# Merge turned round: the ungated sums of the two-input branch first, with Strassen pairs, the gated branch last; HGRN gates at the head of the late stage

## The chip, the cores and the metric

The kernel runs on one core of a Trainium2 chip. TensorE (PE) multiplies matrices; VectorE (DVE), ScalarE (ACT) and GpSimd (POOL) work on tiles in the on-chip memory; SyncE (SP) and POOL issue most of the DMA transfers. Time is device time of one launch, in microseconds (us). The kernel before took 2472.12 us, the median of three runs (2466.22, 2472.12 and 2474.85).

## The reference

One layer of a hybrid decoder step is computed, for 1024 prompt positions and 8 samples. From a normalised input h come the columns of an HGRN2 branch, of a Mamba-2 branch (SSD), and two planes of merge gates. What matters here is the end of the two branches and their merge (cut from the reference):

```python
o_hg = _rmsnorm(o_hg, p['hg_norm']) * jax.nn.silu(og)
...
y = y.reshape(Bsz, T, SSM_INNER) * jax.nn.silu(z)
y = _rmsnorm(y.reshape(Bsz, T, SSM_GROUPS, SSM_INNER // SSM_GROUPS), p['ssm_norm'])
...
u = (jax.nn.sigmoid(ga + bma) * (o_hg @ p['w_br_a'])
     + jax.nn.sigmoid(gb + bmb) * (y @ p['w_br_b']))
x = x + g1 * (u @ p['w_out'])
...
x = x + g2 * (jnp.square(jax.nn.relu(h2 @ p['w_up'])) @ p['w_down'])
```

D_MODEL is 1024, SSM_INNER is 2048: o_hg has 1024 features, y has 2048, and so `w_br_b` has twice the inputs of `w_br_a`.

## The kernel before

**Planes.** Activations lie transposed: a plane is 128 features on the partitions by NT = 1032 positions (1024 and 8). A matrix of 1024 features is KD = 8 planes, y is 16. Each operand is split into a high and a low part (`hi`, `lo`; `wh`, `wl` for weights), and a product is three matmuls: high by low, low by high, high by high. The split costs an ACT copy and a DVE subtraction for each plane and each weight block.

**Two ways to multiply.** `dense` makes one output plane from 8 input planes: 3 column parts of 344, times 8 planes, times 3 matmuls, 72 in all (line 90). `strassen_pair` makes two output planes from 8 input planes in 7 products of half size instead of 8: 7 products, 2 column quarters of 258, 4 planes, 3 matmuls, 168 in all (line 1314). It needs sums of quarters of the input (`T`, made once for several pairs by `differences` and a split) and sums of quarters of the weights (`strassen_weights`, line 1259, for each pair), and its evacuations add a kept product to another on DVE. `DenseK` makes one or two planes with the input planes in the outer loop, so that it can start before all of them are there.

**Late stage.** `phase_late` makes, from h, the HGRN output gates `og` (8 planes) and the SSD gates `z` (16 planes) in twelve Strassen pairs, in the order og, z, z, four times over; then one pair and one block of merge gates. Beside each pair, the pair before it is finished: `og_post` multiplies o by a row scale (`ybc`, broadcast from DRAM, line 1165) and by silu(og) (line 1166), and stores o to `od` (line 1167). `z_post` multiplies y by silu(z) (line 1176), makes a row scale, and one pair later applies it and stores y to `yd` (line 1190). The loads of o, ybc and y, and the stores of od, are issued by POOL (lines 1200, 1201, 1208). They use the six buffers of pool E, of which the `T` planes hold two; og, z and the merge gates use the four of pool D.

**Merge.** `phase_merge` starts with the gated branch `w_br_a`: 8 planes, each multiplied into a sigmoid gate `u` (line 962), the first two by one `DenseK` that takes planes of o as they come. Then come the 8 planes of the first half of `w_br_b` and the 8 of the second half (lines 990 and 991: gate times sum, added to `u`), the first two of the second half again by a `DenseK`. 24 output planes, all dense; every `w_br_b` sum is multiplied by its gate when it leaves PSUM, in both halves. `phase_out` multiplies by `w_out`.

**Feed-forward.** `phase_ffn` has a down projection of four chunks of 8 input planes. Chunks 0 to 2 are 3 dense planes, two Strassen pairs and 1 dense plane each; meanwhile the operand sums are made from planes loaded a second time (`operands`), and the planes of the next chunk are loaded and split (`load_split_in`, lines 925 to 927) ahead of the last dense plane.

**What sets the order.** The program is written in one thread; a scheduler keeps each engine's order by priorities (`high_priority(AHEAD)` moves weight loads, weight splits and evacuations ahead). An engine works through its queue in that order and waits at an instruction whose input is not there, with all behind it. Buffers come from pools with a fixed number of tiles for each tag (`LATE` maps tags to pools); a load waits until the former user of its buffer is done.

Of the kernel before, what the change touches and what calls it, by code (L numbers as in the profile page):

```python
# [7 lines left out]
F32 = mybir.dt.float32  # L8
# [9 lines left out]
P = 128  # L18
T = 1024
# [899 lines left out]
def load_split_in(k, src, tag):  # L919
# [5 lines left out]
    nc.sync.dma_start(raw, src)  # L925
    nc.scalar.activation(hi, raw, AF.Copy)
    nc.vector.tensor_tensor(lo, raw, hi.bitcast(F32), op=ALU.subtract)
    return hi, lo
# [26 lines left out]

def phase_merge(k):

    nc = k.nc
    u, y1, y2, gb = [], [], [], []

    def mul(m):
        return lambda s, ps: nc.vector.tensor_tensor(u[m][:, cs(s)], u[m][:, cs(s)], ps, op=ALU.mult)
    raw = [k.pp.tile([P, NT], F32, tag="L", name="or") for _ in range(4)]
    with k.tc.high_priority(AHEAD):
        for i in range(4):
            nc.sync.dma_start(raw[i], k.od[i])
    d = DenseK(k, (k.i["w_br_a"][0], k.i["w_br_a"][1]), (mul(0), mul(1)))
    oX = []
    for i in range(KD):
        with k.tc.high_priority(AHEAD):  # L970
            oX.append(split_plane(k, raw[i], "A") if i < 4 else load_split(k, k.od[i], "A"))
            if i == 7:
                k.kept = k.hi
                k.late()
            if i == 3:
                u += [load_gate(k, m, "Q1", k.hi) for m in range(2)]
        d.step(*oX[i])
    for m in range(2, KD):
        u.append(load_gate(k, m, "Q1", k.hi if m < 4 else None))
        dense(k, k.i["w_br_a"][m], oX, mul(m))  # L980
        y1.append(load_split(k, k.yd[m - 2], "Q3" if m < 6 else "Q2"))
    y1 += [load_split(k, k.yd[m], "Q2") for m in range(6, KD)]
    for m in range(KD):
        gb.append(load_gate(k, KD + m, "A"))
    order(k, nc.scalar.preload_act_table_set("natural_log_exp_and_others"), k.sigmoid)

    def evac1(m):
        def f(s, ps):
            t = k.sp2.tile([P, SW], F32, tag="mt", name="mt", bufs=2)
            nc.vector.tensor_tensor(t, gb[m][:, cs(s)], ps, op=ALU.mult)  # L990
            nc.vector.tensor_tensor(u[m][:, cs(s)], u[m][:, cs(s)], t, op=ALU.add)
        return f
    for m in range(KD):
        dense(k, k.i["w_br_b"][m], y1, evac1(m))
        if m < 4:
            y2.append(load_split(k, k.yd[KD + m], "A"))
    uX = []
    for m in range(KD):
        tag = "Q3" if m < 4 else "A"
        hi = k.pp.tile([P, NT], F32R, tag=tag, name="uh")  # L1000
        lo = k.pp.tile([P, NT], F32R, tag=tag, name="ul")
        uX.append((hi, lo))

    def evac2(m):
        add = evac1(m)
        hi, lo = uX[m]

        def f(s, ps):
            add(s, ps)
            uu = u[m][:, cs(s)]  # L1010
            nc.scalar.activation(hi[:, cs(s)], uu, AF.Copy)
            nc.vector.tensor_tensor(lo[:, cs(s)], uu, hi[:, cs(s)].bitcast(F32), op=ALU.subtract)
        return f
# [43 lines left out]
def phase_out(k, uX):  # L1057
# [3 lines left out]
    for m in range(KD):  # L1061
        x1.append(k.pp.tile([P, NT], F32, tag="Q1", name="x1"))
        nc.sync.dma_start(x1[m], k.i["xT"][m])
    h2 = []
    for m in range(KD):
        tag = "A" if m < 4 else "Q2"
        h2.append((k.pp.tile([P, NT], F32R, tag=tag, name="h2h"),
                   k.pp.tile([P, NT], F32R, tag=tag, name="h2l")))
# [31 lines left out]
def late_planes(k, T, i):  # L1100

    nc = k.nc
    a, b = [k.pp.tile([P, NT], F32, tag="D", name=n) for n in ("ta", "tb")]
    for x, (xh, xl) in ((a, k.hX[i]), (b, k.hX[i + 4])):
        nc.vector.tensor_tensor(x, xh.bitcast(F32), xl.bitcast(F32), op=ALU.add)
    differences(k, a, b)
    for x, ts in ((a, (1, 3)), (b, (4, 2))):
        p = split_plane(k, x, "T", "th", "tl")
        for n, t in enumerate(ts):
            T[t].append(tuple(y[:, n * HN:(n + 1) * HN] for y in p))  # L1110
# [9 lines left out]
def phase_late(k, gates):  # L1120
# [74 lines left out]
    for n in range(12):  # L1195
        if n % 3 == 0:
            j = n // 3
            og, o, ybc = planes("D", "og"), planes("E", "o"), planes("E", "ybc")
            for a in range(2):
                nc.gpsimd.dma_start(o[a], k.od[2 * j + a])  # L1200
                nc.gpsimd.dma_start(ybc[a], k.rh[2 * j + a].broadcast_to([P, NT]))
            strassen_pair(k, [k.i["w_hg"][(2 * j + a) * 4 + 1] for a in range(2)], X, pair(og))
            beside(k, og_post(og, j, o, ybc))
        else:
            g = n // 3 * 2 + n % 3 - 1
            z, y = planes("D", "z"), planes("E", "y")
            for a in range(2):
                nc.gpsimd.dma_start(y[a], k.yd[2 * g + a])
            strassen_pair(k, [k.i["w_ssm"][g * 6 + 4 + a] for a in range(2)], X, pair(z))
            beside(k, z_post(z, g, y))  # L1210
# [5 lines left out]
    finish(k)  # L1216
    gate_block(k, next(gates), "D", True)
# [3 lines left out]
def strassen_planes(k, h2, T, i):  # L1221

    nc = k.nc
    a, b = stage(k), stage(k)
    for x, (xh, xl) in ((a, h2[i]), (b, h2[i + 4])):
        nc.vector.tensor_tensor(x, xh.bitcast(F32), xl.bitcast(F32), op=ALU.add)  # L1230
    differences(k, a, b)
    for x, tag, ts in ((a, "A", (1, 3)), (b, "Q3", (4, 2))):
# [97 lines left out]
def phase_ffn(k, x1, h2):  # L1330
# [55 lines left out]
    spare = []  # L1386

    def shape(c):
        return 3, 2 if c < 3 else 0

    def operands(c, T, i):
        tags = "A%d" % (c % 2), "Q3" if c % 2 else "Q2"
        if i == 0:
            spare[:] = [[k.pp.tile([P, NT], F32, tag=t, name="ar") for t in tags] for _ in range(2)]
        ps = [[k.pp.tile([P, NT], F32R, tag=t, name=n) for n in ("th", "tl")] for t in tags]
        raw = spare[i % 2] if i < 3 else [stage(k) for _ in ps]
        for n, r in enumerate(raw):
            nc.sync.dma_start(r, ad[c * KD + i + 4 * n])
        differences(k, *raw)
        for (hi, lo), r, ts in zip(ps, raw, ((1, 3), (4, 2))):  # L1400
            nc.scalar.activation(hi, r, AF.Copy)
            nc.vector.tensor_tensor(lo, r, hi.bitcast(F32), op=ALU.subtract)
            for n, t in enumerate(ts):
                T[t].append(tuple(y[:, n * HN:(n + 1) * HN] for y in (hi, lo)))

# [12 lines left out]
    for c in range(4):  # L1418
        T = {n: [] for n in (1, 2, 3, 4)}
        ahead, pairs = shape(c)  # L1420
        for m in range(ahead):
            for i in ((0, 1), (2,), (3,))[m] if pairs else ():
                operands(c, T, i)
            dense(k, down[c * KD + m], aX, add(m))
        X = strassen_operands(aX, T) if pairs else None
        for n in range(pairs):
            m = ahead + 2 * n
            strassen_pair(k, [down[c * KD + m + a] for a in range(2)], X, add_pair(m))
        if c == 3:
            break  # L1430
        nX = [act(c + 1, i) for i in range(KD)]
        for m in range(ahead + 2 * pairs, KD):
            dense(k, down[c * KD + m], aX, add(m), 2)
        aX = nX
    M0 = 3
    free = [k.pp.tile([P, NT], F32R, tag=t, name="free") for t in ("A1", "Q3") for _ in range(8)]
# [20 lines left out]
LATE = {"A": ("A0",) * 8 + ("A1",) * 8, "T": ("L",) * 14 + ("E",) * 2, "Q1": ("L",) * 8, "Q2": ("D",) * 4 + ("E",) * 4, "Q3": ("E",) * 2 + ("L",) * 6}  # L1457
# [22 lines left out]
def body(ctx, tc, ins, outs):  # L1480
# [30 lines left out]
    with tc.tile_pool(name="pl", bufs=1) as pl, tc.tile_pool(name="sp2", bufs=1) as k.sp2:  # L1511
        k.pp.add(pl, L=14)
# [122 lines left out]
```

## Time and profile before

| What | Value |
|---|---|
| runs (median) | 2466.22, 2472.12, 2474.85 (2472.12) us |
| the profiled execution: time | 2468.79 us |
| its span | 2466.9 us |
| granted TensorE clock, mean | 0.997 |
| late stage's thirteen pairs | from 1106.7 to 1386.2 us |
| merge's planes of `w_br_a` after its first two, and of the first half of `w_br_b` | from about 1423.5 us on |
| feed-forward's chunk passage, used as a pattern | 2171 to 2192 us |

The time of the profiled execution is the one that sums from the trace stand against; it lies 3.3 us below the median. A busy share is the engine's busy time over the span. In rows of a timeline stand the start, the duration, engine, line, operation, output and inputs, and in brackets how long the engine was idle before and what released it; "L90" is line 90 of the kernel before.

### The profile page before, as it was taken

What the parts mean: (1) busy time and instruction counts of PE and PEld (TensorE: products, weight loads), DVE (VectorE), ACT (ScalarE), POOL (GpSimd) and SP (SyncE); (2) the same over time, 40 slices, a digit from 0 to 9 for tenths busy, and PEclk for the clock granted to TensorE, in tenths of its full rate; (3) what the DMA queues carried; (4) which work ended last, traced back from release to release, by engine and by line L of the source; (5) the groups of instructions that cost most, each with busy time, mean ns of one, the idle gap of its engine ahead of it and who ended that gap; (6) DMA issues with size and microseconds to landing.
All of it is one profiled execution on the core that took longest, in us unless ns stands there. A gap on an engine that the chain in (4) does not pass through costs nothing.

```text
span 2466.9 us, 51549 instructions
## 1 busy us (share of the span) xinstructions
PE 2429.1 (98%) x21918; PEld 2365.5 (96%) x21918; DVE 1685.2 (68%) x2953; ACT 1118.9 (45%) x1789; POOL 112.7 (5%) x218
## 2 busy tenths in 40 slices
PE   8999999999999999999999999999999999999998
PEld 7999999999999999999999999999999999999997
DVE  7656666459888788886777644356976666786755
ACT  4444454466665556535556523123533334343331
POOL 0000000000000000000111000000012222000000
PEclk9999999999999999999999999999999999999999
DMA  6333333334545454533555744223333335354231
GB/s 262 122 114 122 107 117 112 123 93 148 174 131 172 142 166 130 186 127 112 181 189 181 249 138 154 69 103 130 99 106 104 106 107 181 124 189 152 81 129 70
DMA packets 111591, 339.39 MB, mean 138 GB/s; under 512 B 20128, under 2 KB 26128, under 8 KB 111344
## 3 DMA queue, kind: packets, MB, share of 16 engines
q1 hardware_dynamic: 94656, 283.23, 34.3%
q0 software_dynamic: 16272, 52.52, 6.1%
q8 instruction: 172, 2.82, 0.5%
q14 instruction: 59, 0.48, 0.1%
q10 hardware_dynamic: 432, 0.35, 0.0%
HBM read 266.45 MB, written 69.85 MB: 136 GB/s over the span
## 4 chain that ended last, share of the span: by engine, by line
PE 84%; DVE 5%; DMA 4%; ACT 3%; issue 3%; POOL 0%; DVEq 0%; ACTq 0%; POOLq 0%
PE acc L90 55%; PE b L1314 17%; PE lv_ps L587 2%; PE y_ps L882 1%; PE kvx_ps L849 1%; PE o_ps L551 1%; PE yi_ps L890 1%; PE acc L141 1%; DMA y<-yd 1%; DMA wr<-od 1%; DVE wl L58 1%; PE ada_ps L205 1%; PE kv_ps L534 1%; DVE wl L1259 1%; PE cb_ps L812 1%
## 5 line engine op out<-in xcount | busy, mean ns | idle before, releaser
L90 PE MATMUL acc<-hl,wh 128*128 128x344 f32 x1608 | 527.6, 328 | 0.1
L90 PE MATMUL acc<-hh,wl 128*128 128x344 f32 x1608 | 516.5, 321 | 0.0
L90 PE MATMUL acc<-hh,wh 128*128 128x344 f32 x1608 | 515.6, 321 | 0.0
L90 PEld LDWEIGHTS acc<-hl,wh 128*128 128x128 f32 x1608 | 302.3, 188 | 5.2 <-issue 2.8
L90 PEld LDWEIGHTS acc<-hh,wh 128*128 128x128 f32 x1608 | 302.5, 188 | 3.9 <-issue 3.9
L90 PEld LDWEIGHTS acc<-hh,wl 128*128 128x128 f32 x1608 | 302.6, 188 | 0.0
L90 PE MATMUL acc<-hi,wl 128*128 128x344 f32 (+3 forms) x888 | 285.2, 321 | 1.9 <-DVE wl L58 1.8
L1314 PE MATMUL b<-th,wl 128*128 128x258 f32 x992 | 281.4, 284 | 5.6 <-DVE wl L1259 5.4
L90 PE MATMUL acc<-lo,wh 128*128 128x344 f32 (+3 forms) x888 | 283.8, 321 | 1.4 <-ACT wh L57 1.4
L90 PE MATMUL acc<-hi,wh 128*128 128x344 f32 (+3 forms) x888 | 284.2, 320 | 0.0
L1314 PE MATMUL b<-tl,wh 128*128 128x258 f32 x992 | 280.4, 283 | 0.0
L1314 PE MATMUL b<-th,wh 128*128 128x258 f32 x992 | 280.2, 283 | 0.0
L57 ACT ACTIVATE wh<-wr 128x1024 fp32r<-128x1024 f32 (+1 forms) x146 | 151.0, 1037 | 218.9 <-PE acc L90 148.3
L58 DVE TENSOR_TENSOR wl<-wr,wh 128x1024 fp32r<-128x1024 f32 (+1 forms) x146 | 175.2, 1201 | 69.2 <-ACT wh L57 68.2
L1314 PEld LDWEIGHTS b<-th,wl 128*128 128x128 f32 x992 | 187.6, 189 | 7.9 <-DVE wl L1259 7.4
L1259 DVE TENSOR_TENSOR wl<-wr,wh 128x512 fp32r<-128x512 f32 (+1 forms) x155 | 139.8, 902 | 77.8 <-ACT wh L1277 45.0
L1314 PEld LDWEIGHTS b<-tl,wh 128*128 128x128 f32 x992 | 187.4, 189 | 4.5 <-issue 4.5
L1314 PEld LDWEIGHTS b<-th,wh 128*128 128x128 f32 x992 | 187.4, 189 | 0.0
L90 PEld LDWEIGHTS acc<-hi,wl 128*128 128x128 f32 x888 | 167.3, 188 | 4.3 <-DVE wl L58 3.3
L90 PEld LDWEIGHTS acc<-lo,wh 128*128 128x128 f32 x888 | 167.0, 189 | 3.4 <-ACT wh L57 2.0
L90 PEld LDWEIGHTS acc<-hi,wh 128*128 128x128 f32 x888 | 167.5, 189 | 0.7
L756 DVE SCALAR_TENSOR_TENSOR cv<-raw,cst,cv 128x1024 f32<-128x1024 f32 x96 | 122.5, 1276 | 0.5
(346 smaller groups left out, 5129.6 us busy)
## 6 DMA issues: line engine op xcount, KB each, us to landing
wr<-w_ssm SPq DMA_DIRECT2D x48, 512.0 KB
wr<-w_ada SPq DMA_DIRECT2D x36, 512.0 KB
lo<-ad SPq DMA_DIRECT2D x32, 516.0 KB
wr<-w_hg SPq DMA_DIRECT2D x32, 512.0 KB
w<-cumd SPq DMA_DIRECT2D x32, 512.0 KB
wr<-w_up SPq DMA_DIRECT2D x32, 512.0 KB
wr<-w_down SPq DMA_DIRECT2D x32, 512.0 KB
ad<-r POOLq DMA_DIRECT2D x96, 129.0 KB, 2.2
```

Of the source, the lines that this page charges most:

```text
L57: nc.scalar.activation(wh[:, c], wr[:, c], AF.Copy)
L58: nc.vector.tensor_tensor(wl[:, c], wr[:, c], wh[:, c].bitcast(F32), op=ALU.subtract)
L90: last = nc.tensor.matmul(acc, a[:, sl], b[:, c], start=(i == 0 and j == 0), stop=(i == n - 1 and j == 2))
L141: k.nc.tensor.matmul(ac[s][:, :SW], a[:, sl], b[:, cs(s)], start=(i == 0 and j == 0), stop=(i == self.n - 1 and j == 2))
L205: nc.tensor.matmul(ps[r, :64], k.scT[:, i, :], w[:, :, r], start=i == 0, stop=i == KD - 1, tile_position=(0, 32 * g))
L534: nc.tensor.matmul(kv[ci // 4][:, ci % 4 * P:(ci % 4 + 1) * P], ktok[:, cc], vtok[:, cc], start=True, stop=True)
L551: nc.tensor.matmul(ps[:, c * P:(c + 1) * P], a, x[:, c * P:(c + 1) * P], start=n == 0, stop=n == len(parts) - 1, skip_group_check=True)
L587: k.nc.tensor.matmul(out, QK[hf][:, HT + key:HT + key + 32], x, start=True, stop=True, tile_position=(0, 32 * g))
L756: nc.vector.scalar_tensor_tensor(cv[:, :T], raw[:, j:j + T], cw[:, j:j + 1], cv[:, :T], ALU.mult, ALU.add)
L812: nc.tensor.matmul(ps[:, c * P:(c + 1) * P], Bc[:, cc], Cc[:, cc], start=True, stop=True)
L1259: nc.vector.tensor_tensor(out, x, y, op=ALU.subtract)
L1314: nc.tensor.matmul(acc, a[:, sl], x[:, cols], start=(p in (1, 7, 2) and i == 0 and j == 0), stop=(i == KD // 2 - 1 and j == 2), skip_group ...
```

## The change

The merge is turned round. The 16 planes of y are multiplied first, in two chunks of 8 input planes, A (y 0 to 7) and B (y 8 to 15). Each chunk now has the form of the feed-forward's chunks: 3 dense planes, two Strassen pairs, 1 dense plane, with operand sums from planes loaded a second time. The sums go to `v` without gates: chunk A puts them there (ACT copy or DVE addition), chunk B adds to them on DVE. Then come the gates of both branches (16 loads and sigmoids), `v` is multiplied by the second gate, and the 8 dense planes of `w_br_a` are multiplied by the first gate, added to `v`, and split for `w_out`. No `DenseK` is left in the merge.

The feed-forward's `operands` becomes `operand_sums`, and its loop over chunks the shared function `chunk`. The late stage runs its four og pairs first and its eight z pairs behind them, and loads the first 8 planes of y (`k.yX`) ahead of its last gate block. Tags are renamed, and pool L's 14 buffers become two pools of 8 and 6.

```diff
+def operand_sums(k, src, T, i, tag, spare):
+    if i == 0:
+        spare[:] = [[k.pp.tile([P, NT], F32, tag=tag + t, name="ar") for t in "ab"] for _ in range(2)]
+    ps = [[k.pp.tile([P, NT], F32R, tag=tag + t, name=n) for n in ("th", "tl")] for t in "ab"]
+    raw = spare[i % 2] if i < 3 else [stage(k) for _ in ps]
+    for n, r in enumerate(raw):
+        nc.sync.dma_start(r, src[i + 4 * n])
+    differences(k, *raw)
+    for (hi, lo), r, ts in zip(ps, raw, ((1, 3), (4, 2))):
+        nc.scalar.activation(hi, r, AF.Copy)
+        k.summed = nc.vector.tensor_tensor(lo, r, hi.bitcast(F32), op=ALU.subtract)
...
+def chunk(k, src, X, ws, evac, evac_pair, tag, following, first=None):
+    T = {n: [] for n in (1, 2, 3, 4)}
+    spare = []
+    for m in range(3):
+        for i in ((0, 1), (2,), (3,))[m]:
+            operand_sums(k, src, T, i, tag, spare)
+        dense(k, ws[m], X, evac(m))
+    if first is not None:
+        k.kept = k.summed
+        first()
+    SX = strassen_operands(X, T)
+    for m in (3, 5):
+        strassen_pair(k, [ws[m], ws[m + 1]], SX, evac_pair(m))
+    out = following()
+    dense(k, ws[7], X, evac(7), 2)
+    return out
...
 def phase_merge(k):
...
-    d = DenseK(k, (k.i["w_br_a"][0], k.i["w_br_a"][1]), (mul(0), mul(1)))
...
-    for m in range(KD):
-        dense(k, k.i["w_br_b"][m], y1, evac1(m))
...
+    w = [[k.i["w_br_b"][c * KD + m] for m in range(KD)] for c in range(2)]
+    y2 = chunk(k, k.yd[:KD], k.yX, w[0], put, put_pair, "S1",
+               lambda: [load_split_in(k, k.yd[KD + i], half_tag("S1", i)) for i in range(KD)], k.late)
+    oX = chunk(k, k.yd[KD:], y2, w[1], add, add_pair, "S0",
+               lambda: [load_split_in(k, k.od[i], half_tag("S0", i)) for i in range(KD)])
+    after = k.hi
+    gates = [[load_gate(k, n, half_tag("S1", m), after) for n in (m, KD + m)] for m in range(KD)]
...
+        nc.vector.tensor_tensor(v[m], v[m], gb, op=ALU.mult)
...
+            u = v[m][:, cs(s)]
+            nc.vector.tensor_tensor(t, ga[:, cs(s)], ps, op=ALU.mult)
+            nc.vector.tensor_tensor(u, u, t, op=ALU.add)
...
     for m in range(KD):
-        dense(k, w[KD + m], y2, evac2(m))
+        dense(k, k.i["w_br_a"][m], oX, merged(m))
...
-    for n in range(12):
-        if n % 3 == 0:
-            j = n // 3
...
+    for j in range(4):
+        og, o, ybc = planes("D", "og"), planes("E", "o"), planes("E", "ybc")
...
+    for g in range(G):
+        z, y = planes("D", "z"), planes("E", "y")
...
+    k.yX = [load_split_in(k, k.yd[i], half_tag("S0", i)) for i in range(KD)]
     gate_block(k, next(gates), "D", True)
```

How the order on an engine moves shows at two places. The first is DVE beside the second pair of the late stage. Before, that pair is a z pair, and its evacuations stand together, with one weight split between them (z is the pair's output, s a kept product, b a PSUM bank, numbers tell buffers apart):

```order
L1259 TENSOR_TENSOR wl_13498<-wr_13481,wh_13497 128x1024
L1146 TENSOR_TENSOR z_13474<-s1_13527,b3_13510 128x258
L1146 TENSOR_TENSOR z_13474<-s1_13541,b3_13511 128x258
L1259 TENSOR_TENSOR wl_13503<-wr_13480,wh_13502 128x512
L1146 TENSOR_TENSOR z_13475<-s7_13555,b1_13506 128x258
L1146 TENSOR_TENSOR z_13475<-s7_13569,b1_13507 128x258
```

In the change it is an og pair, and the row-scale multiplications of its own second plane and of the next pair's first plane (L1198) stand among its evacuations:

```order
L1290 TENSOR_TENSOR wl_13502<-wr_13485,wh_13501 128x1024
L1198 SCALAR_TENSOR_TENSOR o_13477<-o_13477,hgn_156,ybc_13479 128x1032
L1179 TENSOR_TENSOR og_13474<-s1_13531,b3_13514 128x258
L1179 TENSOR_TENSOR og_13474<-s1_13545,b3_13515 128x258
L1290 TENSOR_TENSOR wl_13507<-wr_13484,wh_13506 128x512
L1179 TENSOR_TENSOR og_13475<-s7_13559,b1_13510 128x258
L1198 SCALAR_TENSOR_TENSOR o_13715<-o_13715,hgn_156,ybc_13717 128x1032
L1179 TENSOR_TENSOR og_13475<-s7_13573,b1_13511 128x258
```

What moved: two multiplications that take a loaded ybc plane, one to the place ahead of the first evacuation, one between the two evacuations of one product.

The second place is ACT at the start of the gated branch. Before, it opens the merge, and four high parts of o stand ahead of the table load and of two sigmoids (gt is a gate, wh a weight's high part, or and lo a loaded plane):

```order
L57 ACTIVATE wh_16540<-wr_16538 128x1024
L156 ACTIVATE hi_16556<-or_16530 128x1032
L156 ACTIVATE hi_16578<-or_16531 128x1032
L156 ACTIVATE hi_16600<-or_16532 128x1032
L156 ACTIVATE hi_16622<-or_16533 128x1032
L950 ACT_TABLE_LOAD
L950 ACTIVATE gt_16626<-gt_16626 128x1032
L950 ACTIVATE gt_16629<-gt_16629 128x1032
```

In the change it is behind chunk B. Here are the last three of o's eight high parts (hi_18238 is plane 2, hi_18263 plane 7, hi_18243 plane 3), and the weight between them is that of the second `w_br_a` plane:

```order
L926 ACTIVATE hi_18238<-lo_18239 128x1032
L926 ACTIVATE hi_18263<-lo_18264 128x1032
L57 ACTIVATE wh_18507<-wr_18505 128x1024
L950 ACT_TABLE_LOAD
L950 ACTIVATE gt_18354<-gt_18354 128x1032
L926 ACTIVATE hi_18243<-lo_18244 128x1032
L950 ACTIVATE gt_18357<-gt_18357 128x1032
```

What moved: a plane of o that the first `w_br_a` plane needs stands behind a weight split, a table load and a sigmoid.

More of the change, by code (lines that the diff above doesn't have):

```diff
@@ L916, in load_split, with load_split_in @@
     return split_plane(k, r, tag)
-def load_split_in(k, src, tag):
+def load_split_in(k, src, tag, queue=None):
     nc = k.nc
@@ L924, in load_split_in @@
     raw = lo.bitcast(F32)
-    nc.sync.dma_start(raw, src)
-    nc.scalar.activation(hi, raw, AF.Copy)
+    k.loaded = (queue or nc.sync).dma_start(raw, src)
+    k.hi = nc.scalar.activation(hi, raw, AF.Copy)
     nc.vector.tensor_tensor(lo, raw, hi.bitcast(F32), op=ALU.subtract)
@@ L953, in load_gate, with half_tag @@
     return t
+def half_tag(tag, i):
+    return tag + "ab"[i // 4]
+def operand_sums(k, src, T, i, tag, spare):
+    nc = k.nc
+    if i == 0:
[8 more added lines that the diff above has]
+        k.summed = nc.vector.tensor_tensor(lo, r, hi.bitcast(F32), op=ALU.subtract)
+        for n, t in enumerate(ts):
+            T[t].append(tuple(y[:, n * HN:(n + 1) * HN] for y in (hi, lo)))
@@ L956, in phase_merge @@
 def phase_merge(k):
     nc = k.nc
[L959 to L966, printed above, removed]
-    d = DenseK(k, (k.i["w_br_a"][0], k.i["w_br_a"][1]), (mul(0), mul(1)))
[L968 to L982, printed above, removed]
-    for m in range(KD):
-        gb.append(load_gate(k, KD + m, "A"))
-    order(k, nc.scalar.preload_act_table_set("natural_log_exp_and_others"), k.sigmoid)
-    def evac1(m):
+    v = []
+    def put(m):
+        v.append(k.pp.tile([P, NT], F32, tag="V", name="v"))
+        return lambda s, ps: nc.scalar.activation(v[m][:, cs(s)], ps, AF.Copy)
@@ new lines, in put_pair, with evac, add @@
+    def put_pair(m0):
+        v.extend(k.pp.tile([P, NT], F32, tag="V", name="v") for _ in range(2))
+        def evac(m, half, q, a, ps):
+            c = half * HN + q * HQ
+            t = v[m0 + m][:, c:c + HQ]
+            if a is None:
+                nc.scalar.activation(t, ps, AF.Copy)
+            else:
+                nc.vector.tensor_tensor(t, a, ps, op=ALU.add)
+        return evac
+    def add(m):
+        return lambda s, ps: nc.vector.tensor_tensor(v[m][:, cs(s)], v[m][:, cs(s)], ps, op=ALU.add)
@@ new lines, in add_pair, with evac @@
+    def add_pair(m0):
+        def evac(m, half, q, a, ps):
+            c = half * HN + q * HQ
+            t = v[m0 + m][:, c:c + HQ]
+            if a is not None:
+                nc.vector.tensor_tensor(t, t, a, op=ALU.add)
+            nc.vector.tensor_tensor(t, t, ps, op=ALU.add)
+        return evac
+    w = [[k.i["w_br_b"][c * KD + m] for m in range(KD)] for c in range(2)]
+    y2 = chunk(k, k.yd[:KD], k.yX, w[0], put, put_pair, "S1",
+               lambda: [load_split_in(k, k.yd[KD + i], half_tag("S1", i)) for i in range(KD)], k.late)
@@ new lines, in phase_merge, with merged @@
+    oX = chunk(k, k.yd[KD:], y2, w[1], add, add_pair, "S0",
+               lambda: [load_split_in(k, k.od[i], half_tag("S0", i)) for i in range(KD)])
+    after = k.hi
+    gates = [[load_gate(k, n, half_tag("S1", m), after) for n in (m, KD + m)] for m in range(KD)]
+    order(k, nc.scalar.preload_act_table_set("natural_log_exp_and_others"), k.sigmoid)
+    uX = []
+    def merged(m):
+        ga, gb = gates[m]
+        nc.vector.tensor_tensor(v[m], v[m], gb, op=ALU.mult)
+        hi, lo = [k.pp.tile([P, NT], F32R, tag=half_tag("S1", m), name=n) for n in ("uh", "ul")]
+        uX.append((hi, lo))
@@ L992, in evac1 @@
         return f
     for m in range(KD):
-        dense(k, k.i["w_br_b"][m], y1, evac1(m))
[L995 to L1013, printed above, removed]
@@ L1061, in phase_out @@
     for m in range(KD):
-        x1.append(k.pp.tile([P, NT], F32, tag="Q1", name="x1"))
+        x1.append(k.pp.tile([P, NT], F32, tag="V", name="x1"))
         nc.sync.dma_start(x1[m], k.i["xT"][m])
@@ L1106, in late_planes @@
     differences(k, a, b)
-    for x, ts in ((a, (1, 3)), (b, (4, 2))):
-        p = split_plane(k, x, "T", "th", "tl")
+    for x, tag, ts in ((a, "S0a", (1, 3)), (b, "S0b", (4, 2))):
+        p = split_plane(k, x, tag, "th", "tl")
         for n, t in enumerate(ts):
@@ L1193, in z_post @@
         pending.append(apply)
-    for n in range(12):
-        if n % 3 == 0:
-            j = n // 3
[L1198 to L1210, printed above, removed]
+    for j in range(4):
+        og, o, ybc = planes("D", "og"), planes("E", "o"), planes("E", "ybc")
+        for a in range(2):
+            nc.gpsimd.dma_start(o[a], k.od[2 * j + a])
+            nc.gpsimd.dma_start(ybc[a], k.rh[2 * j + a].broadcast_to([P, NT]))
+        strassen_pair(k, [k.i["w_hg"][(2 * j + a) * 4 + 1] for a in range(2)], X, pair(og))
+        beside(k, og_post(og, j, o, ybc))
+    for g in range(G):
+        z, y = planes("D", "z"), planes("E", "y")
+        for a in range(2):
+            nc.gpsimd.dma_start(y[a], k.yd[2 * g + a])
+        strassen_pair(k, [k.i["w_ssm"][g * 6 + 4 + a] for a in range(2)], X, pair(z))
+        beside(k, z_post(z, g, y))
     ns = [next(gates) for _ in range(2)]
@@ L1231, in strassen_planes @@
     differences(k, a, b)
-    for x, tag, ts in ((a, "A", (1, 3)), (b, "Q3", (4, 2))):
+    for x, tag, ts in ((a, "S1a", (1, 3)), (b, "S1b", (4, 2))):
         p = split_plane(k, x, tag, "th", "tl")
@@ L1385, in phase_ffn @@
         dense(k, up[j], h2, evac_up(j))
[L1386 to L1404, printed above, removed]
     def add_pair(m0):
@@ L1418, in phase_ffn @@
     for c in range(4):
[L1419 to L1428, printed above, removed]
+        ws = [down[c * KD + m] for m in range(KD)]
         if c == 3:
+            for m in range(M0):
+                dense(k, ws[m], aX, add(m))
             break
[L1431 to L1436, printed above, removed]
+        aX = chunk(k, ad[c * KD:(c + 1) * KD], aX, ws, add, add_pair, "S1" if c % 2 else "S0",
+                   lambda: [act(c + 1, i) for i in range(KD)])
+    free = [k.pp.tile([P, NT], F32R, tag=half_tag("S1", i // 2), name="free") for i in range(16)]
     ws = [load_w(k, down[3 * KD + m], tiles=None if m < M0 + 2 else [free[2 * (m - M0) - 4 + n][:, :KD * P] for n in range(2)])
```

24 lines of the change are left out of this document (8 added, 16 removed).

## The prediction

> **What bounds the kernel now.** I read the page's totals first, then the chain that ended last, then single stages.
>
> ```profile
> span 2466.9 us, 51549 instructions
> PE 2429.1 (98%) x21918; PEld 2365.5 (96%) x21918; DVE 1685.2 (68%) x2953; ACT 1118.9 (45%) x1789; POOL 112.7 (5%) x218
> PE 84%; DVE 5%; DMA 4%; ACT 3%; issue 3%; POOL 0%; DVEq 0%; ACTq 0%; POOLq 0%
> ```
>
> TensorE (PE) is busy for 98% of the span, and 84% of the chain is its own. So time changes in two ways only: fewer or shorter matmuls, or PE stalls that come or go. DVE at 68% is an average; what it does to PE shows in single places. The stages that the change touches, in the view by windows (columns: window, its length, busy time of PE, PEld, DVE, ACT and POOL, granted clock, DMA share, GB/s):
>
> ```profile
> 1106.70:1386.20 279.50, 273.26 (x2234) 264.84 (x2233) 198.18 (x270) 163.68 (x256) 35.09 (x66) 1.00 0.49 165
> 1386.20:1423.50 37.30, 35.22 (x221) 34.36 (x220) 20.61 (x22) 22.43 (x24) 2.12 (x4) 1.00 0.84 302
> 1423.50:1606.00 182.50, 181.76 (x1152) 181.29 (x1152) 71.57 (x103) 43.81 (x44) 0.00 (x0) 1.00 0.37 119
> ```
>
> The first is the late stage with its 13 Strassen pairs, the second the passage into the merge, the third sixteen dense planes of the merge (16 x 72 = the 1152 matmuls): PE is busy for 181.76 of 182.50 us, with nothing left to hide. PE's waits, first in the late stage (1100 to 1400), then in the merge (1386 to 1700; "us in total, times, longest us"):
>
> ```profile
> PE b L1314 <- DVE wl L1259: 6.0, 5, 2.1
> ```
> ```profile
> PE acc L90 <- DVE wl L58: 1.5, 2, 0.8
> PE acc L90 <- ACT wh L57: 1.4, 2, 0.7
> PE acc L141 <- ACT gate L937: 0.8, 1, 0.8
> ```
>
> So 6.0 us in the late stage and 3.7 in the merge are all that better ordering could win there. More must come from fewer matmul columns.
>
> **Part 1: eight dense planes become four Strassen pairs.** The chain of waits gives the pace of each kind, in stretches where PE waits for nothing (start, us, count):
>
> ```profile
> 1423.52 158.47 PE acc L90 x1005
> 1838.10 61.98 PE b L1314 x518
> ```
>
> A matmul of 344 columns takes 158.47 / 1005 = 0.1577 us, and a dense plane of 72 takes 11.35 us. One of 258 columns takes 61.98 / 518 = 0.1197 us, and a pair of 168 takes 20.10 us. Eight dense planes at 90.8 us go and four pairs at 80.4 us come: **-10.4 us**. The new work on DVE and ACT (differences and splits of operands, and two additions for each product kept) is what the feed-forward's down projection does beside the same matmuls; the second row is from that projection, so its pace includes such neighbours. Ends: nothing gained if operands came late throughout, -10.4 if never. I take -10.4.
>
> **Part 2: the late stage in a new order.** Today's waits there have one form:
>
> ```profile
> 1207.82 1.06 POOL L1208 DMA_DIRECT2D y<-yd  x2 [5.51 <-DMA yd<-y]
> 1213.59 1.23 DVE L1176 TENSOR_TENSOR y<-y,z 128x1032 f32<-128x1032 f32 x1 [1.52 <-DMA y<-yd]
> 1215.48 0.39 PE L1314 MATMUL b<-th,wl 128*128 128x258 f32 x1 [1.36 <-DVE wl L1259]
> ```
>
> The load of y gets its buffer only after an HGRN pair (og) has taken the E buffers, y lands 5.7 us later, DVE stands 1.52 us in front of the product, and the weight split behind it (L1259) is late for PE. This happens at the three places where an SSD pair (z) follows an og pair; two of 0.5 us follow at z to og. Between two z pairs there is none. With four og pairs first and eight z pairs behind, the alternation goes and with it **-6.0 us**.
>
> What comes is og after og, which before never has. Its price is built from these rows:
>
> ```profile
> 1128.81 0.55 POOL L1167 DMA_DIRECT2D od<-o  x1 [11.72 <-DVE o L1166]
> 1131.28 0.53 POOL L1167 DMA_DIRECT2D od<-o  x1 [1.93 <-DVE o L1166]
> 1134.08 0.54 POOL L1208 DMA_DIRECT2D y<-yd  x1 [2.26 <-DMA od<-o]
> 1135.51 0.54 POOL L1208 DMA_DIRECT2D y<-yd  x1 [0.90 <-DMA od<-o]
> ```
> ```profile
> 1206.25 1.29 DVE L1165 SCALAR_TENSOR_TENSOR o<-o,hgn,ybc 128x1032 f32<-128x1032 f32 x1 [2.37 <-DMA ybc<-rh]
> ```
> ```profile
> DMA to landing us min/median/max: 4.2/6.3/7.4
> ```
>
> The E pool has six buffers, two of them held by operand sums, so of an og pair's four planes (two o, two ybc) the next pair's last two wait for a buffer. The second pair began at 1126.9: its stores of the pair before go out at +1.9 and +4.4 us, and 5.3 us after a store its buffer takes the next load (1128.81 to 1134.08). So the freed buffer takes a ybc load at +7.2. It lands 4.2 to 7.4 us later (last row, the tile view of ybc); DVE multiplies 1.29 us; that frees a ybc buffer, the second ybc load is issued at +12.9 to +15, lands at +17.1 to +21.3, DVE multiplies again. In the new order this second multiplication stands on DVE between two evacuations of one product (0.4 us each), so the later one ends at +18.8 to +23.0 us. PE wants that bank for the second half of the seventh product, at +18.7 (six products of 20.10 / 7 = 2.87 us, and half of one). That is a stall of 0.1 to 4.3 us, 1.6 in the middle, for the second and third og pair; the first has fresh buffers (0.3 taken) and the fourth one plane less to fetch (none). Sum +3.5. **Late stage: -6.0 + 3.5 = -2.5 us**, ends -5.5 (no stall in the chain) and +3 (both stalls at 4.3). If all loads landed at 7.4 us it would be nearer +6.
>
> **Part 3: the passages of the merge.** The old 3.7 us go. Three passages are new: late stage to chunk A, A to B, and B to the gated branch. All three load eight planes in front of a dense plane and split them on ACT and DVE. The feed-forward's chunks do just this:
>
> ```profile
> 2187.61 1.08 ACT L926 ACTIVATE hi<-lo 128x1032 fp32r<-128x1032 f32 x1 [1.46 <-DMA lo<-ad]
> 2189.72 1.06 ACT L57 ACTIVATE wh<-wr 128x1024 fp32r<-128x1024 f32 x1 [1.03 <-PE acc L90]
> ```
> ```profile
> 2190.28 1.22 DVE L927 TENSOR_TENSOR lo<-lo,hi 128x1032 fp32r<-128x1032 f32 x1
> ```
>
> The next dense plane starts at 2189.25 and PE does not wait: the last plane is split at 2191.5, the time at which its matmuls come. The first two passages have the same form, but at each one high part stands behind a weight split that waits for PE, so I take 0.5 and 0.7 us.
>
> At the third, ACT's order is: weight split of the second gated plane (it waits, like the 2189.72 row, until 0.47 us into the dense plane), a table load, the first gate's sigmoid, and only then the high part of o plane 3. Their durations:
>
> ```profile
> 1392.92 1.28 ACT L950 ACT_TABLE_LOAD   x1
> 1394.21 2.02 ACT L950 ACTIVATE gt<-gt 128x1032 f32<-128x1032 f32 x2
> ```
>
> From the start of that dense plane: weight split done at 0.47 + 1.06 = 1.53, table 2.8, sigmoid 3.8, high part 4.9, low part on DVE 6.1 us. PE reaches plane 3 after 9 matmuls, 9 x 0.158 = 1.4 us. So it stalls **4.7 us**; the ends are 0 (if ACT gets through its queue ahead of the dense plane's end) and 7 (if the gate's load, issued ahead of o plane 3, lands 2.3 us late too).
> The table's price is open to a second reading. The Trainium skill, "ScalarE: Activation LUTs", section "What ACT_TABLE_LOAD costs", says that a switch costs a drain of some 1.4 us besides the load of about 1.28 us. This trace agrees on the load and shows no drain: the next row on ACT starts 0.01 us after it. By the page the stall would be some 6.1 us.
>
> Merge: 0.5 + 0.7 + 4.7 - 3.7 = **+2.2 us**. The sixteen gate loads of 516 KB lie beside the eight dense planes (4.13 MB each half, where the 182.50 us row above moved 119 GB/s at a DMA share of 0.37), and per plane DVE has 7.2 us to do in 11.35. Both cost nothing while that cover holds.
>
> A stall can also cost twice, through the clock:
>
> ```profile
> 1604.00:1608.00 4.00, 2.48 (x15) 1.90 (x14) 3.88 (x8) 2.54 (x5) 0.00 (x0) 1.00 0.00 0
> 1608.00:1612.00 4.00, 4.00 (x17) 4.00 (x17) 4.00 (x9) 1.34 (x3) 0.00 (x0) 0.57 0.37 133
> ```
>
> After a window in which PE worked 2.48 of 4 us, the granted clock fell to 0.57 over the next 4 us: about 3.4 us at half speed, 1.7 us lost. This place (the two planes computed together in the old merge) goes, and the 4.7 us stall is a new one of the kind: 1.7 - 1.7 = 0.
> The Trainium skill, "TensorE: Matmul & The Clock Gate", section "Part 1: The HAM clock gate", puts the fall at an idle window of about 3.4 us. Here PE had idled only some 1.5 us in its window, so the trace shows a fall after less; by the page the old place would have cost nothing and the new stall would bring its 1.7 us.
>
> **Part 4: the rest.** The feed-forward calls the shared chunk code with the same work in the same order, and the output stage changes buffer tags only: 0, with 1.5 us either way for shifted loads.
>
> **Sum:** -10.4 - 2.5 + 2.2 = -10.7 us, against the profiled run's 2468.79: 2458.1. That run lies 3.3 us below the median of the three, 2472.12, so against the median 2461.4, say **2461**.
>
> **The rivals.**
> - A, the forecast, 2455 to 2467 by the ends of parts 2 and 3: chance 0.55.
> - B, the orders bite less: og chain without stalls, the gated branch's stall about 1 us because ACT runs ahead: -10.4 - 6.0 - 3.7 + 1 = -19, 2453. For it: the feed-forward's passages show no stall. Against: the table load and sigmoid stand ahead of o plane 3 in the program. 0.18.
> - C, a new wait replaces the old: ybc at 7.4 us in each of the chain's links, both stalls near 4.3 and as much again behind them (12 us): -10.4 - 6 + 12 + 2.2 = -2.2, 2470. For it: DVE already waited 2.37 us for one ybc. 0.12.
> - D, the clock falls at two more passages: 2 x 1.7 us on A, 2465. 0.06.
> - E, slower: loads at the passages aren't hidden. Eight planes are 4.13 MB; at the late stage's 165 GB/s that is 25 us, and without a head start 25 + 2.3 (split) - 11.35 (dense plane ahead) - 3.3 (plane 7 is wanted 21 x 0.158 us in) = 12.7 us. At the late and the gated passage: 25.4 in place of the 5.2 counted, 2481. It decides once both pass 8 us. Against: 302 GB/s in the row of the second window, at which the passage costs 1.3 us. 0.06.
> - F, the change does less than it says: pairs in the merge run at the late stage's mean, 279.50 / 13 = 21.5 us (with its 50 other matmuls and waits): 4 x 1.4 us less, 2467. 0.03.
>
> **How the numbers follow.** Likeliest is A, 2461. The range must hold 0.8: A whole, B mostly and C's near part: 2450 to 2470. Below 2464.7 (0.3% under the median, about what a measurement of this kernel can tell) lie 0.45 of A's 0.55, B and 0.02 of D: 0.65. Slower is E, 0.06. The rest, 0.29, is the same.
>
> **What would show it.** PE rows in the merge: sixteen dense planes and four pairs of 20.1 us; if pairs take more, part 1 is wrong. No DVE wait for a y load in front of PE in the late stage; a DVE wait for ybc in the og pairs of 0 to 4 us. One PE stall of 4 to 6 us a microsecond or two into the first gated plane, released by DVE's low part of o plane 3, and a granted clock near half behind it. The forecast is wrong if gate or plane loads end later than PE wants them, or if feed-forward time moves by more than 1.5 us.

## The result, and the profile after

The change takes **2454.30 us**, the median of six runs (2451.30 to 2456.04); before, beside it, 2471.61 us. The ratio is **0.9930, with a 95% interval of 0.9916 to 0.9943**: 17 us faster, from 14 to 21. Two later comparisons of the same two kernels gave 0.9937 (0.9920 to 0.9954) and 0.9928 (0.9913 to 0.9943). The prediction was 2461, 10.7 us faster.

The page after, its totals and the chain that ended last by engine:

```profile
span 2454.1 us, 51952 instructions
PE 2419.3 (99%) x22014; PEld 2355.8 (96%) x22014; DVE 1736.0 (71%) x3019; ACT 1155.7 (47%) x1859; POOL 112.7 (5%) x218
PE 49%; DVE 2%; DMA 2%; ACT 1%; issue 1%; SPq 0%; DVEq 0%; POOL 0%; ACTq 0%; POOLq 0%
```

PE's share rises to 99% and its busy time falls by 9.8 us, about the four pairs' gain; the other 3.0 us between the two spans are waiting that went. (The chain of this kernel is followed back only as far as 1142 us, so its shares don't stand against those of before.) The windows after (columns as before): the late stage, two Strassen pairs of chunk A, and a passage with four dense planes:

```profile
1108.90:1383.10 274.20, 272.80 (x2235) 264.29 (x2233) 196.95 (x270) 165.16 (x258) 34.09 (x64) 1.00 0.50 171
1434.40:1474.60 40.20, 40.20 (x336) 40.20 (x335) 17.89 (x28) 14.76 (x28) 0.00 (x0) 1.00 0.27 91
1474.80:1520.20 45.40, 45.40 (x290) 45.29 (x289) 38.72 (x48) 20.74 (x24) 0.00 (x0) 1.00 0.56 198
```

PE works throughout both pairs: 20.10 us each, as forecast. Its waits after, in the late stage (1100 to 1400; the waits of the last gate block in it are left to the next fence) and from the passage to the merge's end (1375 to 1700):

```profile
PE b L1345 <- DVE og L1179: 0.9, 2, 0.7
```
```profile
PE acc L90 <- DVE lo L927: 2.5, 2, 2.0
PE acc L141 <- DVE wl L58: 1.7, 1, 1.7
PE acc L90 <- ACT gate L937: 1.6, 1, 1.6
PE acc L141 <- ACT wh L57: 0.2, 1, 0.2
```

The 6.0 us of the late stage are 0.9, the merge's 3.7 are 6.0. Where the time went, from the traces of this study (us). The boundaries are starts of PE's matmuls: the first of the late stage's pairs, the first of the last gate block, the first that sums squares in the output stage (L1053 in the kernel before), and the first of the up projection's Strassen pairs. The sum of squares comes late, so the column "gate block and merge" holds the output stage's first 33.4 to 33.6 us too, in every trace; in differences they drop out.

| Trace | start of late stage | late stage | gate block and merge | output stage | feed-forward to end |
|---|---|---|---|---|---|
| before | 1106.74 | 279.52 | 323.42 | 128.25 | 629.00 |
| before, again | 1106.18 | 282.14 | 323.00 | 128.25 | 627.85 |
| late stage alone | 1107.02 | 273.68 | 321.03 | 128.42 | 628.87 |
| merge alone (old late stage) | 1108.85 | 281.37 | 315.88 | 128.50 | 626.79 |
| the change, dense chunks | 1106.60 | 274.09 | 325.33 | 128.51 | 627.97 |
| the change | 1108.93 | 274.15 | 315.72 | 128.46 | 626.84 |
| the change, again | 1107.75 | 272.71 | 314.02 | 128.45 | 626.81 |
| the change, third | 1107.31 | 273.33 | 316.55 | 128.45 | 626.75 |
| + loads of passage 1 | 1108.61 | 273.24 | 311.24 | 128.45 | 626.75 |
| + order of passage 3 | 1107.29 | 273.59 | 314.20 | 128.44 | 627.01 |
| + both | 1106.93 | 273.18 | 311.81 | 128.45 | 626.88 |
| + both, again | 1106.74 | 274.78 | 312.05 | 128.43 | 626.56 |
| + both and weight split | 1106.30 | 273.72 | 310.69 | 128.45 | 627.63 |

By the means of the three traces with the old late order and of the three of the change, the late stage loses 7.6 us (281.0 to 273.4); the merge, from two traces of before to three of the change, 7.8 (323.2 to 315.4); the feed-forward 1.6. Together -16.8 with the output stage, which fits the ratio. The first two traces alone differ by 12.8 us: the late stage began 2.2 us later in one of them, though the program is the same up to there.

### The profile page after: what moved, and what is told of

It reads as the page before. It is cut to its first block, busy times and chain, and to the rows that moved or that the text cites. A ratio compares the mean times of both kernels' runs of the same rounds, so it can differ in the third digit from the quotient of the medians.

```text
span 2454.1 us, 51952 instructions
## 1 busy us (share of the span) xinstructions
PE 2419.3 (99%) x22014; PEld 2355.8 (96%) x22014; DVE 1736.0 (71%) x3019; ACT 1155.7 (47%) x1859; POOL 112.7 (5%) x218
## 4 chain that ended last, share of the span: by engine, by line
PE 49%; DVE 2%; DMA 2%; ACT 1%; issue 1%; SPq 0%; DVEq 0%; POOL 0%; ACTq 0%; POOLq 0%
PE b L1345 26%; PE acc L90 22%; DMA ybc<-rh 1%; DVE wl L58 0%; DMA lo<-yd 0%; DMA lo<-od 0%; ACT wh L57 0%; PE ss L567 0%; PE ss L1087 0%; DVE lo L927 0%; DVE ht L1116 0%; DVE sqa L1080 0%; DMA lo<-ad 0%; DVE x L1453 0%; DVE h2l L1118 0%
## 5 line engine op out<-in xcount | busy, mean ns | idle before, releaser
L1345 PE MATMUL b<-th,wl 128*128 128x258 f32 x1120 | 317.4, 283 | 0.3
L1345 PE MATMUL b<-tl,wh 128*128 128x258 f32 x1120 | 317.3, 283 | 0.0
L1345 PE MATMUL b<-th,wh 128*128 128x258 f32 x1120 | 315.9, 282 | 0.0
L90 PE MATMUL acc<-lo,wh 128*128 128x344 f32 (+3 forms) x792 | 254.0, 322 | 4.1 <-DVE lo L927 2.5
L90 PE MATMUL acc<-hi,wl 128*128 128x344 f32 (+3 forms) x792 | 254.5, 321 | 0.1
L90 PE MATMUL acc<-hi,wh 128*128 128x344 f32 (+3 forms) x792 | 253.5, 320 | 0.0
L1345 PEld LDWEIGHTS b<-tl,wh 128*128 128x128 f32 x1120 | 211.5, 189 | 4.5 <-issue 4.5
L1345 PEld LDWEIGHTS b<-th,wl 128*128 128x128 f32 x1120 | 211.6, 189 | 2.7 <-DVE wl L1290 2.7
L1345 PEld LDWEIGHTS b<-th,wh 128*128 128x128 f32 x1120 | 211.4, 189 | 0.0
L90 PEld LDWEIGHTS acc<-hi,wh 128*128 128x128 f32 x792 | 149.4, 189 | 0.8
```

The lines of the kernel that those rows point to most:

```text
L90: last = nc.tensor.matmul(acc, a[:, sl], b[:, c], start=(i == 0 and j == 0), stop=(i == n - 1 and j == 2))
L1345: nc.tensor.matmul(acc, a[:, sl], x[:, cols], start=(p in (1, 7, 2) and i == 0 and j == 0), stop=(i == KD // 2 - 1 and j == 2), skip_group ...
```

## The experiments

**Which parts of a trace repeat.** The kernel before, unchanged.

> The kernel before, unchanged, for a second trace: which parts of a trace repeat. Up to the late stage (the program before it is the same in both kernels) the trace of the change runs 2.2 us behind that of before. Theory 'chance': the late stage begins anywhere within 2 us of 1106.7, and the feed-forward's 1.6 us stall at 1918 may be missing. Theory 'the kernel': 1106.7 within 0.3 us, and the stall stands at the same place.

2469.19 us; the late stage begins at 1106.18, while it begins between 1106.3 and 1108.9 in the others: chance. But the feed-forward's stall stood at the same place again, 80.4 us behind that projection's first pair, with 1.1 us. So one part of each theory held.

The change itself, twice more:

> The change, unchanged, for a second trace and more times. Theory 'chance in single runs': its late stage begins within 2 us of 1108.9, its stalls at the passages stand at the same places (1.9 and 1.8 us in the last gate block, 0.7 and 2.1 us in the first gated plane), and the median gain is 13 to 19 us. Rival: the stalls at the passages vary by as much as the medians and the traces differ (4 us).

> The change once more, for times beside the two that follow. Its 6 to 8 us less in the merge and 7 to 8 us less in the late stage repeat; median ratio to before 0.992 to 0.995. Theory 'half clock by chance': its stalls of about 2 us stand at the same four places, while 3.2 us stretches at half clock follow none, one or two of them. Rival: the half-clock stretch always follows the same stall.

Medians 2451.85 and 2453.60. The stalls at the passages, read from one matmul's start to the next, repeat (1.9, 2.1 and 2.1 us; 1.8, 1.7 and 2.5; 2.1 in all three). The stretches of 3.15 us at half clock do not: one, none, one.

**The late stage alone**, and **the merge alone**. The first edit puts the new loops into the kernel before, the second the old loop into the change:

```diff
-    for n in range(12):
-        if n % 3 == 0:
...
+    for j in range(4):
+        og, o, ybc = planes("D", "og"), planes("E", "o"), planes("E", "ybc")
...
+    for g in range(G):
```

> The kernel before with the new order of the late stage alone (og pairs first), the old merge. Theory 'late stage': the two parts of the change are independent, so this gains what the traces show of the late stage, 279.5 - 274.1 = 5.4 us, and PE waits for about 1 us in the og pairs. By the prediction's sum it would gain 2.5 us. Rival 'needs the new merge': the gain is lost at the passage into the old merge, because the last z pairs now end later than the old merge's first loads want; time as before, within 1.5 us.

> The change with the old order of the late stage (og, z, z). Theory 'late stage': 5.4 us slower than the change, and the three stalls of 1.5 to 2.3 us in front of the first z after an og are back. Rival: the stalls were those of a chance run and time is that of the change.

Late stage alone: 2462.81 against 2469.45 us, ratio 0.9972 (0.9962 to 0.9982). Merge alone: 2462.81, ratio 0.9976 (0.9966 to 0.9986). Each is worth some 6 to 7 us by itself, the two together 16 to 17; their product, 0.9948, lies above the change's ratio, and the intervals don't say whether the two are quite independent. PE's waits in the late stage, first of the new order in the old kernel, then of the old order in the new:

```profile
PE b L1311 <- DVE og L1146: 0.5, 1, 0.5
```
```profile
PE b L1348 <- DVE wl L1293: 7.0, 6, 3.5
```

The wait belongs to the order, not to the merge: 6.0, 7.4 and 7.0 us in the three traces with og, z, z; 0 to 1.4 in those with og first. That the gain is lost at the old merge's passage is refuted: that merge was 2 us shorter than in the two traces of before.

**Dense chunks.** The Strassen pairs and their operand sums are left out of both merge chunks; seven dense planes in a row and the eighth behind the loads:

```diff
-        for i in ((0, 1), (2,), (3,))[m]:
+        for i in ((0, 1), (2,), (3,))[m] if evac_pair else ():
...
+    if evac_pair is None:
+        for m in range(3, 7):
+            dense(k, ws[m], X, evac(m))
+        out = following()
+        dense(k, ws[7], X, evac(7), 2)
+        return out
```

> The change with eight dense planes in each merge chunk, without Strassen pairs and without their operand sums. Theory 'matmul columns': 10.4 us slower than the change (4 pairs of 20.1 us against 8 planes of 11.35). If operand loads cost the change time at the late passage, up to 3.5 us of that comes back: 7 to 10.4 us slower. Rival 'order': most of the gain is the turned-round order (no planes made two at a time), and this is less than 4 us slower.

2464.51 us, 10.9 above the median of the 18 runs of the change (2453.60), and 10.4 to 12.6 by the ratios to the kernel before; the merge is 9.9 us longer in the trace (325.3 against the mean 315.4). The matmul columns carry the merge's gain; the turned-round order brings none of it. That the trace comes so near to 10.4 is helped by two things that nearly cancel: this trace has two stretches at half clock (1.4 us lost in each; see the last section), where the three of the change have 0.7 in the mean, and it has no stall at the third passage, where those have 2.5 to 2.8 us. The stalls at the first passage were there too (1.9 and 1.8 us), though no operand loads were.

**The first passage: loads.** In the change the last plane's high part is late on ACT, and the gate block's evacuation waits behind it. SP's queue and ACT, then the windows:

```profile
1375.88 4.13 SPq L925 DMA_DIRECT2D lo<-yd  x4
1383.85 0.32 SPq L968 DMA_DIRECT2D ar<-yd  x1
1384.26 0.91 SPq L925 DMA_DIRECT2D lo<-yd  x2
1385.52 0.93 SPq L968 DMA_DIRECT2D wr<-yd  x1
1386.51 0.71 SPq L925 DMA_DIRECT2D lo<-yd  x1
```
```profile
1398.26 1.06 ACT L926 ACTIVATE hi<-lo 128x1032 fp32r<-128x1032 f32 x1 [1.79 <-DMA lo<-yd]
1399.23 0.97 ACT L937 ACTIVATE gate<-acc,cst 128x344 f32<-128x344 f32 x2
```
```profile
1396.00:1400.00 4.00, 2.40 (x15) 1.98 (x14) 2.49 (x3) 2.21 (x5) 0.00 (x0) 1.00 0.85 349
1400.00:1404.00 4.00, 4.00 (x17) 3.78 (x17) 4.00 (x6) 2.10 (x3) 0.00 (x0) 0.66 0.48 149
```

SP stands from 1380.0 to 1383.9 at an operand load (`ar`); two plane loads (`lo`) stand behind it, and a third behind the next operand load (`wr<-yd`). PE waits 1.75 us for the evacuation, and this time half clock follows. The edit orders chunk A's operand loads behind the plane loads:

```diff
     for n, r in enumerate(raw):
-        nc.sync.dma_start(r, src[i + 4 * n])
+        d = nc.sync.dma_start(r, src[i + 4 * n])
+        for l in k.lds if len(k.lds) == KD else ():
+            order(k, d, l)
```

> The change with chunk A's operand loads put behind all eight plane loads on SP's queue. Theory 'queue': in the trace of the change SP stood from 1380.0 to 1383.9 at an operand load whose buffer PE still read, with three plane loads behind it; with these first the stall of 1.75 us in the last gate block goes, and the 3 us at half clock behind it: 3.4 us faster. Rival 'bandwidth': the transfers fill the DMA engines there (share 0.85 to 1.0, 350 to 400 GB/s), so the last plane lands as late as before: same within 0.7 us. Second rival: the stalls move to the operand sums, later in chunk A.

SP's queue with the edit, and PE's waits (1375 to 1700):

```profile
1374.69 6.13 SPq L925 DMA_DIRECT2D lo<-yd  x7
1382.77 8.74 SPq L970 DMA_DIRECT2D ar<-yd  x2
```
```profile
PE acc L141 <- DVE wl L58: 1.9, 1, 1.9
PE acc L90 <- DVE lo L929: 1.7, 1, 1.7
```

Seven planes go out in one piece and the wait for the evacuation (L937) is gone, here and in the three later traces with this edit; the merge takes 311.2 us. Counted from the gate block's first matmul, the last plane's high part begins after 9.2 us instead of 15.2, so the rival, under which it would land as late as before, is refuted: the order on SP's queue made it late. The edit also takes the operand transfers out of the planes' way, and no run separates that from the waiting on SP. In the dense variant, which has no operand loads, SP stood at a weight load instead, with plane loads behind it, and the stall was there all the same. The times could not tell this single edit from the change beside it (2451.57 against 2451.85).

**The third passage: order.** The edit puts all of o's high parts ahead of the sigmoids and all loads of o ahead of the gate loads:

```diff
-    after = k.hi
+    after = k.his[-KD:], k.lds[-KD:]
...
-        order(k, k.sigmoid, after)
+        for h, l in zip(*after):
+            order(k, k.sigmoid, h)
+            order(k, d, l)
```

> The change with all high parts of o ahead of the table load and the sigmoids on ACT, and all loads of o ahead of the gate loads on SP. Theory 'queue on ACT': the stall of 2.1 us in the first gated plane goes (o plane 3's high part is 2.35 us earlier), 1.5 to 2.1 us faster. Rival 'landing': o plane 3 is issued at 1568.8 and lands some 7 us later, so its high part cannot start much before 1576: 0.4 us faster at most. Second rival: the gate comes later by that and the first evacuation waits: no gain.

The change has this on SP, ACT, DVE and PE at that place (`gt` is a gate; the `lo` load is plane 3 of o):

```profile
1568.46 0.32 SPq L949 DMA_DIRECT2D gt<-gd  x1
1568.83 0.44 SPq L925 DMA_DIRECT2D lo<-od  x1
```
```profile
1573.37 1.04 ACT L57 ACTIVATE wh<-wr 128x1024 fp32r<-128x1024 f32 x1
1574.43 1.28 ACT L950 ACT_TABLE_LOAD   x1
1575.73 1.07 ACT L950 ACTIVATE gt<-gt 128x1032 f32<-128x1032 f32 x1
1576.70 1.05 ACT L926 ACTIVATE hi<-lo 128x1032 fp32r<-128x1032 f32 x1
```
```profile
1577.78 1.23 DVE L927 TENSOR_TENSOR lo<-lo,hi 128x1032 fp32r<-128x1032 f32 x1 [1.62 <-ACT hi L926]
```
```profile
1579.07 0.43 PE L90 MATMUL acc<-lo,wh 128*128 128x344 f32 x1 [1.98 <-DVE lo L927]
```

With the edit SP and ACT run like this, and PE's waits follow:

```profile
1562.61 1.38 SPq L925 DMA_DIRECT2D lo<-od  x3
```
```profile
1572.30 1.06 ACT L926 ACTIVATE hi<-lo 128x1032 fp32r<-128x1032 f32 x1
1573.38 1.28 ACT L952 ACT_TABLE_LOAD   x1
```
```profile
PE acc L90 <- ACT gate L939: 1.9, 1, 1.9
PE acc L141 <- DVE wl L58: 1.9, 1, 1.9
PE acc L90 <- DVE lo L929: 0.5, 2, 0.3
```

The high part now follows the weight split, and the stall falls from 2.1 to 0.4 us. The queue on ACT is only a part of this. In the change SP waited 3.5 us at the gate load, whose buffer PE still read, with plane 3's load behind it; that load landed at 1575.83 (last semaphore update in the trace), only 0.9 us before the high part began, and 0.9 and 1.7 us before it in the other two traces of the change. So the order on ACT alone could not have taken away more than that; the rest comes from the load, which now goes out ahead of the gate loads and lands at 1571.62. The edit moves both orders at once, and no run separates them; the rival 'landing' was right that the landing stood close behind. Median 2450.78.

**Both edits, and one more.**

> Both edits together. If both queue theories hold: 5 us faster than the change. If only the first: 3.4 us. If both are bandwidth: the same time.

> Both edits of the passages together, once more, since the first times left it open whether the shorter stalls show. Theory 'stalls are time': trace 3.3 us shorter in the merge than the change (1.7 and 1.7 us of stall), median 2 to 5 us lower. Rival: what the passages gain is lost elsewhere, median within 1 us of the change.

Medians 2449.89 and 2450.41, ratios 0.9925 (0.9910 to 0.9940) and 0.9917 (0.9903 to 0.9932). Over all runs: 2450.24 (12 runs) against 2453.60 for the change (18 runs), 3.4 us less, about what the two stalls came to (some 3.7 us); in the two comparisons where both kernels ran side by side it was 2.0 and 3.2. The last kernel moves the weight split of the gate block ahead of that of y plane 0:

```diff
+    for i in range(KD):
+        if i != 7:
+            order(k, k.his[i], k.wh)
```

> Both edits, and the last gate block's weight split ahead of y plane 0's split on ACT, and so on DVE. In all traces of the change PE stood 1.9 to 2.1 us in the first planes of that gate block, waiting for its weight's low part, which stood on DVE behind the low part of y plane 0. Theory 'queue on DVE': that wait shortens by one subtraction, 1.15 us, to 0.9 us. Rival: the evacuations of the gate pair hold DVE until the same time, no change. Median 0 to 2 us below the kernel with two edits.

2448.38 us, ratio 0.9909 (0.9895 to 0.9923): the fastest of all kernels here, ahead of both. Its reason is not shown, though:

```profile
PE acc L90 <- DVE lo L929: 1.5, 2, 1.3
PE acc L141 <- DVE wl L58: 1.5, 1, 1.5
PE b L1354 <- DVE gate L1181: 0.4, 1, 0.4
```

The wait for the weight falls from 1.9 to 1.5 us only, since the evacuations of the gate pair hold DVE until then (the rival), and 0.4 us come up in front of it. At the third passage the first stall is 1.3 us in this trace, where both edits alone had 0.2 to 0.4. But its merge and late stage hold no stretch at half clock, while each trace of both edits alone has one; that is 1.4 us by itself, and may be chance. The interval overlaps with that of both edits alone.

## Why the prediction was right or wrong

**Part 1, the Strassen pairs: right.** -10.4 us forecast; a pair takes 20.10 us, and without the pairs the merge is 9.9 us longer by trace, 10.9 by medians.

**Part 2, the late stage: right in its mechanism, wrong in two sizes**, -2.5 us against -7.6. The old waits were put at the 6.0 us of one trace; they are 6.0, 7.0 and 7.4, and twice a half-clock stretch followed them (before, again, at 1347 us; merge alone, at 1349). The larger miss is the new og chain, +3.5 us. It runs as described:

```profile
1136.30 0.53 POOL L1232 DMA_DIRECT2D ybc<-rh  x1 [2.32 <-DMA od<-o]
1137.59 0.53 POOL L1231 DMA_DIRECT2D o<-od  x1 [0.76 <-DMA od<-o]
1142.26 0.53 POOL L1232 DMA_DIRECT2D ybc<-rh  x1 [4.13 <-DVE o L1198]
```
```profile
1146.72 1.29 DVE L1198 SCALAR_TENSOR_TENSOR o<-o,hgn,ybc 128x1032 f32<-128x1032 f32 x1 [3.16 <-DMA ybc<-rh]
```

With the pair beginning at 1129.1, the ybc loads go out at +7.2 and +13.2 us, where the prediction put +7.2 and +12.9 to +15. But they land in 4.5 us, not in the 4.2 to 7.4 that the old order showed. The tile view of ybc, of the change and then of the change with the old late order:

```profile
DMA to landing us min/median/max: 4.3/5.1/5.7
```
```profile
DMA to landing us min/median/max: 4.8/6.3/7.3
```

With 4.5 us at both loads the prediction's own chain ends at +19.2 us, a stall of 0.5. The price of a load was taken from an order in which it stood among y loads; in the new order it isn't there. Over all traces the median landing of ybc is 6.2 to 6.3 us in the three with og, z, z and 4.5 to 5.2 in the ten with og first; that the y loads are the reason is not shown by itself. The chain's range was also added up unevenly: 4.2 to 7.4 us were named for a landing, but its upper end, 4.3 us of stall, takes 6.3 for each, and with 7.4 it is 6.3. The chain stalls PE for 1.2 us in the first trace, for nothing worth naming in the second and third.

**Part 3, the passages: near in their sum by luck, wrong in their places.** Forecast 0.5, 0.7 and 4.7, together 5.9 us; measured in the three traces 3.6 to 4.6, none, and 2.5 to 2.8, together 6.3 to 7.3. One passage was forecast too cheap, the others too dear, and the misses cancel.
- At the first passage "the first two passages have the same form" failed: here operand loads with buffers still in use stand on SP among the plane loads, and a weight split stands on DVE behind a plane's. Moving the loads showed the first; the second stays as read from the trace.
- At the third "PE reaches plane 3 after 9 matmuls" failed. PE's own order takes planes 0 to 2 for all three column parts first, so 27 matmuls, 4.3 us, pass before plane 3:

```
L90 MATMUL acc_18472<-hi_18238,wh_18408 128x344
L90 MATMUL acc_18412<-lo_18244,wh_18408 128x344
```

(acc_18412 is the first column part, acc_18472 the third; lo_18244 is plane 3.) With its own 6.1 us for the low part, the prediction would have said 1.8; 2.1 was measured, but not along that sum. The low part ended 7.1 us after the dense plane's start (at 1571.92), because the weight split on ACT began 1.0 us later than forecast, behind two high parts whose planes landed late; and PE had by then stood 0.65 us for plane 2. The order on ACT was right to the instruction, but plane 3's load, held back on SP by a gate load, landed only 0.9 us ahead of its turn there. The table load took 1.28 us, and the next activation began 0.02 us later: the drain of the Trainium skill ("ScalarE: Activation LUTs", "What ACT_TABLE_LOAD costs") does not show, so 1.4 us more would have been wrong.
- "1.7 - 1.7 = 0" for the clock: near enough in the mean, but not as reasoned. The stretch did not follow the third passage's stall in any trace of the change; in the trace of the merge alone it did, after a stall of the same 2.1 us.

**Part 4: off by more than it allowed.** The feed-forward lost 1.6 us in the mean, up to 2.2. It is one stall in the up projection, where DVE waits for a store to land that frees a buffer, before and after:

```profile
1917.79 0.42 DVE L1370 TENSOR_TENSOR r<-s,b 128x258 f32<-128x258 f32 x1 [4.08 <-DMA ad<-r]
```
```profile
1904.78 0.42 DVE L1401 TENSOR_TENSOR r<-s,b 128x258 f32<-128x258 f32 x1 [1.88 <-DMA ad<-r]
```

It stood in all four traces without Strassen pairs in the merge (1.6, 1.1, 1.3 and 0.5 us) and in none with them. Why the store lands earlier is open.

Rival B (2453) named the right time, in part for the right reason: no stalls in the og chain. It had the gated passage at 1 us and no stall elsewhere; both are wrong. C, E and F are refuted by the traces. D's fall of the clock came at one passage in two of the change's three traces, at 1.4 us. The likeliest case missed the time by 7 us: 5 in the late stage, 1.6 in the feed-forward, and the rest within what the passages vary.

## What to carry to other kernels

Take the order of PE's own matmuls as they stand, not as the loops are written, before asking when an operand is wanted. A DMA queue is a queue: a load that waits for its buffer holds back all that is behind it, so place the loads whose buffers are free first. And price a load in a new order by the traffic of that order; where an order goes, the landing times that it caused go with it.

## What was not expected of the hardware

The same stall is sometimes followed by a stretch at half clock and sometimes not. The stall at the start of the last gate block (1.6 to 2.1 us) stands in all ten traces with the new merge, and half clock followed it directly in four (old late stage, dense chunks, both edits twice). Each time the stretch was eleven matmuls in 3.15 us, which otherwise take 1.74: 1.4 us lost, at a granted clock of 0.50. The Trainium skill, "TensorE: Matmul & The Clock Gate", "Part 1: The HAM clock gate", tells of a window that runs freely; that would give such chance, and these runs agree as far as they go. They show the fall after stalls of some 2 us, less than the window of some 3.4 us. Single runs of one kernel lie up to 12 us apart, and up to three such stretches stand between 1100 and 1700 us of a trace. That they are part of the spread is not shown run by run, but the clock goes with it: of 49 runs of the kernel before, the ten with a mean granted clock of 0.995 have a median of 2472.5 us, the sixteen with 0.997 one of 2466.2.
